# Sums of squares of the RMS norms: columns of TensorE products, in place of running additions on VectorE and GpSimd

## The chip, the core and the metric

The kernel runs on one core of a Trainium2 chip. The metric is the device time of one execution in microseconds; a kernel's time is the median of several runs. The engines are called as in the profile: PE (TensorE), PEld (its weight loads), DVE (VectorE), ACT (ScalarE), POOL (GpSimd), and SP, whose queue issues nearly all loads.

## What is computed

Two layers over 1024 latent tokens of width 1024, with 256 context tokens. Only the opening matters here: both token streams are normalised by their root mean square, then scaled and shifted by vectors that come from two conditioning vectors.

```python
def rmsnorm(x, g):
    xf = x.astype(jnp.float32)
    y = xf * lax.rsqrt(jnp.mean(xf * xf, axis=-1, keepdims=True) + RMS_EPS)
    return (y * g.astype(jnp.float32)).astype(x.dtype)
...
shift, scale, gate = jnp.split(sc @ mod_w[l] + mod_b[l], 3, axis=-1)
hx = modulate(rmsnorm(x, norm_g[l]), shift[:, None], scale[:, None])
...
shift_c, scale_c, gate_c = jnp.split(scc @ mod_w[l] + mod_b[l], 3, axis=-1)
hc = modulate(rmsnorm(ctx, norm_g[l]), shift_c, scale_c)
```

## The kernel before

Everything is held transposed: the 1024 features lie on 8 tiles of 128 partitions, the tokens along the free axis. `x_0` to `x_7` are 128x1024 tiles (two halves of 512 tokens); the context fills `cx_0` and `cx_1`, each four features' tiles of 256 tokens side by side. A sum over features is thus a sum over the 8 tiles and then over the partitions.

The opening does four things at once. (1) `fold`: PE multiplies two groups of the second layer's weights; each group has four pieces (0 to 3) of 24 products of 128x512 per column half. A weight piece is loaded (`wr_wu`), cast by ACT to `wh_wu` (L95) and its rest formed by POOL in `wl_wu` (L96); ACT copies the result out (`fo`, L254) and SP stores it. `gh` and `gl` are the group's other operand; those of the second group take the buffers of the first. (2) `modulation(k)`: DVE forms scale and shift of tile k as dot products of loaded rows `mod` (L212, L216, L220); PE forms those of tiles 6 and 7 (`mod_row`: products `modr`, L322, and transposes `modt`, L328). (3) The sums of squares. (4) `modulate(k)`: DVE multiplies each half of x by the scale and by the reciprocal root (L338), ACT adds the shift into `h0h` (L341), and DVE forms the rest `h0l` (L342). After that PE starts the first projection, `xb` (L126 to L128), which reads `h0h` and `h0l` of all eight tiles; the rest of the program follows from there.

The sums of squares before: ACT squares every half of a tile (L298, into one of four buffers `t`). The halves 0 are added to `ssq0` by POOL, the halves 1 to `ssq1` by DVE (L299); the context's eight pieces of 256 tokens are all added to `ssqc` by POOL. For x, `rstd_cols` then takes the sum over partitions as columns: four PE products with one column of `ones` as the moving operand (L193) put 128 tokens each on the partitions; ACT takes the root and DVE the reciprocal of 128x4 numbers; DVE spreads them on a diagonal `dg_x` (L197), and a product with `ones` (L200) brings them back along the free axis, the same on each partition. For the context, `rstd` multiplies `ones` by `ssqc` (L181), and takes root and reciprocal on 128x256 (L183, L184); `ctx_scale` multiplies `cx` by it (L382), POOL scales and shifts it (L349) and it is split for the projection `xbc`.

The code is not the order of execution: when the program is built, a scheduler places the instructions of each engine by its own estimate of time, and every engine then runs its list in that order. Loads (`load`) are chained, so they are issued in the order of the code. All products in float32 (those with `ones`, `modr`, `modt`) show two records per product in the trace, those in the rounded type one.

Of the kernel before, what the change touches and what calls it, by code (L numbers as in the profile page):

```python
# [9 lines left out]
F32 = mybir.dt.float32  # L10
F32R = mybir.dt.float32r
AF = mybir.ActivationFunctionType
# [3 lines left out]
P = 128  # L16
S = 1024
C = 256
E = C + S
D = 1024  # L20
KT = D // P
H = 512
HALF = (slice(0, H), slice(H, S))
# [32 lines left out]
def body(ctx, tc, xT, ctxT, cc, ccol, modT, modW, win, gw, wout, wu, grp, wg, wo1, small, edge, ident, outT):  # L56
    nc = tc.nc
    mult, add, sub = ALU.mult, ALU.add, ALU.subtract
# [19 lines left out]
    def xtile(name, dt=F32):  # L78
        return xpool.tile([P, S], dt, tag="x", name=name)

    def ttile(name):
        return tpool.tile([P, H], F32, tag="t", name=name)

    def atile(name):
        return apool.tile([P, NR * PW], F32, tag="acc", name=name)

    def psum(name):
        return pm.tile([P, H], F32, tag="mm", name=name)


    def wide(name, n):
        return pc.tile([P, S], F32, tag=("cv", "xb")[n % 2], name=name)
# [8 lines left out]
    def load(out, src):  # L101
        with ExitStack() as lctx:
            if chain[0] is not None:
                lctx.enter_context(tc.issue_after(chain[0].ins))
            d = nc.sync.dma_start(out, src)
            if chain[0] is not None:
                chain[0] = d
# [36 lines left out]
    ones = base.tile([P, P], F32, name="ones")  # L144
    nc.vector.memset(ones, 1.0 / D)
    eps_r = base.tile([P, 1], F32, name="eps_r")
# [31 lines left out]
    def rstd(acc, eps, name, wn=0):  # L178
        n = acc.shape[-1]
        ps = psum(f"ms_{name}") if n < H else wide(f"ms_{name}", wn)  # L180
        nc.tensor.matmul(ps[:, :n], ones, acc, start=True, stop=True)  # L181
        rt = ttile(f"sq_{name}")
        nc.scalar.activation(rt[:, :n], ps[:, :n], AF.Sqrt, bias=eps)  # L183
        nc.vector.reciprocal(acc, rt[:, :n])  # L184


    def rstd_cols(acc, name, idD, rpool, wn):
        n = acc.shape[-1]
        nt = n // P
        ps = wide(f"ms_{name}", wn)  # L190
        r = rpool.tile([P, H // P], F32, tag="rc", name=f"rc_{name}")[:, :nt]
        for c in range(nt):
            nc.tensor.matmul(ps[:, c : c + 1], acc[:, c * P : (c + 1) * P], ones[:, 0:1], start=True, stop=True)  # L193
        nc.scalar.activation(r, ps[:, :nt], AF.Sqrt, bias=eps_r)
        nc.vector.reciprocal(r, r)
        t = ttile(f"dg_{name}")[:, :n]
        nc.vector.tensor_tensor(out=t.rearrange("p (c t) -> p c t", t=P),  # L197
                                in0=idD.unsqueeze(1).to_broadcast([P, nt, P]),
                                in1=r.unsqueeze(2).to_broadcast([P, nt, P]), op=mult)
        nc.tensor.matmul(ps[:, H : H + n], ones, t, start=True, stop=True)  # L200
        return ps[:, H : H + n]
# [66 lines left out]
    with ExitStack() as sctx:  # L268
        fpool = sctx.enter_context(tc.tile_pool(name="fpool", bufs=6))
        gpool = sctx.enter_context(tc.tile_pool(name="gpool", bufs=4))  # L270
        spool = sctx.enter_context(tc.tile_pool(name="spool", bufs=1))
# [14 lines left out]
        cx = [spool.tile([P, D], F32, name=f"cx_{i}") for i in range(2)]  # L286


        xs = []
        acc = [atile("ssq0"), atile("ssq1")]  # L290
        accc = spool.tile([P, C], F32, name="ssqc")

        def sumsq(acc_, v, n, first, name, eng):
            if first:
                nc.scalar.activation(acc_[:, :n], v, AF.Square)
            else:
                q = ttile(name)
                nc.scalar.activation(q[:, :n], v, AF.Square)  # L298
                eng.tensor_tensor(out=acc_[:, :n], in0=acc_[:, :n], in1=q[:, :n], op=add)  # L299

        junk = spool.tile([P, D], F32, name="junk")

        def modulation(k):
            for m in (k, KT + k):
                raw = dtile(f"mod0_{m}")
                load(raw, modT[0, m])
                mod_tile(m0, 0, m, raw, (cL, cC), junk)
            mod_scale(m0, a0, 0, k)
# [3 lines left out]
        idx = spool.tile([P, P], F32, name="idx")  # L312
# [43 lines left out]
        def x_load(k):  # L356
            t = xtile(f"x_{k}")
            load(t, xT[k])
            xs.append(t)
            for h in range(2):  # L360
                sumsq(acc[h], t[:, HALF[h]], H, k == 0, f"xsq_{k}_{h}", nc.vector if h else nc.gpsimd)

        for i in range(2):
            chain[0] = nc.sync.dma_start(cx[i][:1], cc[i : i + 1])
# [3 lines left out]
        for i, t in enumerate((cL, cC)):  # L368
            ps = wide(f"c_{i}", i)
# [2 lines left out]
            nc.scalar.activation(t, ps, AF.Silu, scale=float(D))  # L372
        def ctx_load(i):
            load(cx[i].rearrange("p (k n) -> p k n", n=C), ctxT[4 * i : 4 * i + 4].rearrange("k p n -> p k n"))
            for q4 in range(4):
                sumsq(accc, cx[i][:, q4 * C : (q4 + 1) * C], C, i + q4 == 0, f"csq_{i}_{q4}", nc.gpsimd)

        def ctx_scale():
            rstd(accc, eps_r, "c")
            for i in range(2):  # L380
                v = cx[i].rearrange("p (k n) -> p k n", n=C)
                nc.vector.tensor_tensor(out=v, in0=v, in1=accc.unsqueeze(1).to_broadcast([P, 4, C]), op=mult)  # L382

        def ctx_split(i):
            for k in range(4 * i, 4 * i + 4):
# [13 lines left out]
        modulation(1)  # L399
        x_load(7)  # L400
        modulation(2)
        rx = [rstd_cols(acc[h][:, :H], f"x{h}", idx, spool, h) for h in range(2)]
        mod_row(1)
        mod_row(0)
        fold_some(2)
# [15 lines left out]
        ctx_load(0)  # L421
        fold_some(1)
        ctx_load(1)
        ctx_scale()
        ctx_split(0)
        ctx_split(1)
# [3 lines left out]
    with ExitStack() as actx:  # L430
# [95 lines left out]
        for j in range(KT):  # L526
            uc = utile(f"uc{j}")

            for src, dst in zip(xb, (uc[:, :C], uc[:, C:])):
                n = src.shape[-1]  # L530
                nc.scalar.activation(dst, src, AF.Identity, bias=col(O_SCB + j), scale=col(O_SCW + 4 * j + 2))
                for k, o in ((0, -2), (1, -1), (3, 1)):
                    a, b = max(0, -o), n - max(0, o)
# [7 lines left out]
            roots, root = (None, None) if state is None else decays(j - 1, state[1])  # L541
            w = wload(win[KT + j], f"vg{j}", nc.gpsimd)
            sg = []
            for h in range(2):
                ps = psum(f"vg{j}_{h}")
                mm3(ps, w, (hh, hl), HALF[h])
                t = ttile(f"sg{j}_{h}")
# [51 lines left out]
    def vtile(name):  # L599
        return vpool.tile([P, H], F32, tag="v", name=name)  # L600
# [16 lines left out]
    def block_sums(b11, b12, b21, b22, t3, eng):  # L617
        eng.tensor_tensor(out=t3, in0=b22, in1=b12, op=sub)
        eng.tensor_tensor(out=b12, in0=b12, in1=b11, op=sub)
        eng.tensor_tensor(out=b11, in0=b22, in1=b12, op=sub)  # L620
        eng.tensor_tensor(out=b21, in0=b21, in1=b11, op=sub)
        return dict(t2=b11, t1=b12, t3=t3, t4=b21, b22=b22)
# [94 lines left out]
    for j in range(KT):  # L717
        w = wload(win[4 * KT + j], f"gb{j}", nc.gpsimd)
        th, tl = d2tile(f"ybh{j}", F32R), d2tile(f"ybl{j}", F32R)
        for h in range(2):  # L720
            ps = psum(f"gb{j}_{h}")
# [49 lines left out]
    for h in range(2):  # L771
        ps = wide(f"mu{h}", h)[:, :H]
        nc.tensor.matmul(ps, ones, lnacc[h][:, :H], start=True, stop=True)
        for j in range(KT):
            v = us[j][:, HALF[h]]
# [177 lines left out]
    for i in range(KH):  # L953
# [3 lines left out]
        t = block_sums(b11, b12, b21, b22, ttile(f"xt3_{i}"), nc.vector)  # L957
# [105 lines left out]
    for m in range(0, NK, 2):  # L1063
# [38 lines left out]
        elif m <= KT:  # L1102
            n = 2 * KT + m - 2
# [187 lines left out]
    wb, _, _ = last_half0(m, wa, ahead)  # L1291
# [4 lines left out]
    first, second = slice(H, H + H // 2), slice(H + H // 2, S)  # L1296
# [26 lines left out]
    q4 = p3(m, wa, c4, whole, HALF[1])  # L1323
# [108 lines left out]
```

## Time and profile before

| | |
|---|---|
| time, median of 3 runs | 1375.69 us (1374.39 to 1378.43) |
| profiled execution, its own time | 1381.07 us |
| its span in the profile | 1379.3 us |
| its mean granted PE clock | 0.974 |
| PE busy | 1295.9 us (94%) |
| DVE busy | 1205.1 us (87%) |
| ACT / POOL busy | 632.7 us (46%) / 363.3 us (26%) |
| first `fold` product / first `xb` product starts | 13.32 us / 93.25 us |

The opening is thus the first 7% of the span. Durations below are those of the one profiled execution, which took 5.4 us more than the median. Where a table gives busy time in a window it also gives the clock that PE was granted there, 1.00 for full and 0.50 for half.

### The profile page before, as it was taken

Reading aid. Unit: us, or ns where it says so; the run is one execution under the profiler, and the core shown is the slowest. Engines: PE = TensorE matmul, PEld = TensorE weight load, DVE = VectorE, ACT = ScalarE, POOL = GpSimd, SP = SyncE. Lnnn points to the kernel's source line nnn. Section 1 sums busy time; section 2 is a strip of 40 time slices with the busy share of each in tenths; the row PEclk is TensorE's granted clock in tenths of the full one; section 3 lists DMA queues with packets and bytes.
Section 4 is the critical chain, followed back from the end, with each engine's and each line's share of the span. In section 5 each row is a group of like instructions: output and inputs, shape, how many; then the busy total and the mean of one; then the engine's idle time right before and its main releaser. Section 6 shows DMA issues by size and latency. Waiting matters only on the chain.

```text
span 1379.3 us, 15637 instructions
## 1 busy us (share of the span) xinstructions
PE 1295.9 (94%) x5664; PEld 1048.2 (76%) x5664; DVE 1205.1 (87%) x1587; ACT 632.7 (46%) x906; POOL 363.3 (26%) x182
## 2 busy tenths in 40 slices
PE   7889989898999799999998999999999999999896
PEld 4468868787777587787887887788888888778685
DVE  7998999999999999998778865999999987876775
ACT  6353644674465542304533544754334344634442
POOL 5173534743473555523320004000000000000002
PEclk9899999999999899999999999999999999999997
DMA  9753011111112113343353646424243334758623
GB/s 354 280 180 119 25 59 54 53 40 61 54 35 72 46 46 130 110 151 135 103 185 122 221 154 205 138 93 151 100 145 123 115 115 132 265 190 275 206 107 123
DMA packets 82866, 181.79 MB, mean 132 GB/s; under 512 B 7778, under 2 KB 27618, under 8 KB 82788
## 3 DMA queue, kind: packets, MB, share of 16 engines
q1 hardware_dynamic: 74340, 176.60, 37.8%
q10 hardware_dynamic: 8448, 4.20, 1.0%
q8 instruction: 44, 0.72, 0.2%
q14 instruction: 34, 0.28, 0.1%
HBM read 136.72 MB, written 44.04 MB: 131 GB/s over the span
## 4 chain that ended last, share of the span: by engine, by line
PE 36%; DVE 10%; DMA 7%; issue 2%; ACT 2%; POOL 1%; POOLq 0%; SPq 0%; DVEq 0%; ACTq 0%
PE ga L127 2%; PE ga L128 2%; PE ga L126 2%; PE wob L127 2%; PE wob L128 2%; PE wob L126 2%; DMA wr_g<-wg 1%; DVE ws L986 1%; DMA yr_t<-y_t 1%; DMA wr_v<-wfold 1%; PE qb_g L666 1%; DVE wq_g L96 1%; PE qb_g L669 1%; PE qb_g L668 1%; DVE wq_wo L96 1%
## 5 line engine op out<-in xcount | busy, mean ns | idle before, releaser
L746 DVE SCALAR_TENSOR_TENSOR conv<-u,sm,conv 128x1013 f32<-128x1013 f32 (+14 forms) x232 | 291.2, 1272 | 6.6 <-ACT conv L738 3.8
L1252 POOL TENSOR_TENSOR o<-x,rr 128x256 f32<-128x256 f32 (+1 forms) x9 | 8.0, 923 | 462.9 <-ACT rr L1240 460.0
L511 ACT ACTIVATE g<-g,sm 128x512 f32<-128x512 f32 (+1 forms) x96 | 58.8, 617 | 110.5 <-PE g L510 108.3
L96 POOL TENSOR_TENSOR wl_wu<-wr_wu,wh_wu 128x1024 fp32r<-128x1024 f32 x16 | 39.4, 2470 | 153.9 <-ACT wh_wu L95 147.7
L463 POOL TENSOR_TENSOR g<-g,uc 128x1280 f32<-128x1280 f32 x16 | 47.5, 2967 | 107.9 <-ACT g L511 65.1
L249 PE MATMUL fold<-gh,wh_wu 128*128 128x512 f32 x128 | 53.0, 416 | 5.7 <-ACT wh_wu L95 5.7
L250 PE MATMUL fold<-gl,wh_wu 128*128 128x512 f32 x128 | 52.4, 409 | 3.2 <-DVE gl L96 3.2
L128 PE MATMUL gb<-h0h,wl_gb 128*128 128x512 f32 x128 | 50.7, 398 | 4.8 <-POOL wl_gb L96 4.8
L126 PE MATMUL vg<-h0h,wh_vg 128*128 128x512 f32 x128 | 52.3, 408 | 2.7 <-ACT g L511 2.1
L251 PE MATMUL fold<-gh,wl_wu 128*128 128x512 f32 x128 | 50.7, 405 | 2.3 <-POOL wl_wu L96 2.3
L128 PE MATMUL xb<-h0h,wl_xb 128*128 128x512 f32 x128 | 50.2, 392 | 2.0 <-POOL wl_xb L96 2.0
L127 PE MATMUL wob<-ybl,wh_wob 128*128 128x512 f32 x128 | 50.5, 395 | 1.2 <-POOL ybl L96 1.2
L465 POOL TENSOR_TENSOR g<-g,th 128x1280 f32<-128x1280 f32 x16 | 46.9, 2948 | 16.8 <-ACT th L449 16.8
L127 PE MATMUL vg<-h0l,wh_vg 128*128 128x512 f32 x128 | 51.2, 400 | 0.0
L126 PE MATMUL gb<-h0h,wh_gb 128*128 128x512 f32 x128 | 50.6, 395 | 0.1
L126 PE MATMUL va<-h0h,wh_va 128*128 128x512 f32 x128 | 50.6, 395 | 0.0
L127 PE MATMUL va<-h0l,wh_va 128*128 128x512 f32 x128 | 50.6, 395 | 0.0
L508 PE MATMUL g<-uh,wh_gw 128*128 128x512 f32 (+1 forms) x96 | 36.3, 379 | 15.1 <-ACT wh_gw L95 6.4
L126 PE MATMUL wob<-ybh,wh_wob 128*128 128x512 f32 x128 | 50.6, 396 | 0.0
L128 PE MATMUL wob<-ybh,wl_wob 128*128 128x512 f32 x128 | 49.9, 391 | 0.7 <-POOL wl_wob L96 0.7
L128 PE MATMUL va<-h0h,wl_va 128*128 128x512 f32 x128 | 50.4, 395 | 0.0
L127 PE MATMUL gb<-h0l,wh_gb 128*128 128x512 f32 x128 | 50.4, 393 | 0.0
(548 smaller groups left out, 4301.1 us busy)
## 6 DMA issues: line engine op xcount, KB each, us to landing
mod<-modT SPq DMA_DIRECT2D x28, 512.0 KB, 5.5
wr_wu<-wu SPq DMA_DIRECT2D x16, 512.0 KB, 3.9
x_part<-xp SPq DMA_DIRECT2D x32, 256.0 KB, 2.4
mod<-modT SPq DMA_DIRECT2D x32, 256.0 KB, 3.3
wr_v<-wfold SPq DMA_DIRECT2D x16, 512.0 KB, 3.7
wr_g<-wg SPq DMA_DIRECT2D x16, 512.0 KB, 5.4
wr_wo<-wo SPq DMA_DIRECT2D x16, 512.0 KB, 4.2
yr_t<-y_t SPq DMA_DIRECT2D x16, 512.0 KB, 6.3
```

The costliest lines, as they stand in the source:

```text
L96: eng.tensor_tensor(out=lo, in0=src, in1=hi.bitcast(F32), op=sub))
L126: nc.tensor.matmul(ps, hi[:, kc], xh[k][:, cols], start=(k == 0), stop=False)
L127: nc.tensor.matmul(ps, hi[:, kc], xl[k][:, cols], start=False, stop=False)
L128: nc.tensor.matmul(ps, lo[:, kc], xh[k][:, cols], start=False, stop=(k == ks - 1))
L249: nc.tensor.matmul(ps, wh[:, kc], gh[i], start=(i == 0), stop=False)
L250: nc.tensor.matmul(ps, wh[:, kc], gl[i], start=False, stop=False)
L251: nc.tensor.matmul(ps, wl[:, kc], gh[i], start=False, stop=(i == 3))
L463: nc.gpsimd.tensor_tensor(out=ius[d], in0=ius[d], in1=uc, op=mult)
L465: nc.gpsimd.tensor_tensor(out=ius[d], in0=ius[d], in1=roots[d], op=mult)
L508: nc.tensor.matmul(ps[:, :n], gwh[:, kc], uh[:, a : a + n], start=True, stop=False)
L511: nc.scalar.activation(t[:, a : a + n], ps[:, :n], AF.Sigmoid, bias=col(ob + d * KT + j))
L746: nc.vector.scalar_tensor_tensor(out=(us[j] if k == 30 else acp)[:, a:b], in0=us[j][:, a + o : b + o], scalar=col(O_CONVW + 31 * j + k), i ...
```

## The change

The running sums `ssq0`, `ssq1` and `ssqc` and their additions are gone. Each squared half goes straight to PE: for each 128 tokens of it one product with one column of `ones`, into a column of its own of one PSUM tile (`sumsq`): 64 columns for x (`ms_x`, 8 per tile) and 16 for the context (`ms_c`). `roots` copies half of the columns out of PSUM by ACT, halves them three times by additions on DVE (128x32, 128x16 and 128x8 results for x; 128x8, 128x4, 128x2 for the context), and takes root and reciprocal. `spread` is the old diagonal and the product with `ones`; the context now goes that way as well, and its squares are taken in four pieces of 512 instead of eight of 256. The factor for the context is read from PSUM.

```diff
-        acc = [atile("ssq0"), atile("ssq1")]
-        accc = spool.tile([P, C], F32, name="ssqc")
-
-        def sumsq(acc_, v, n, first, name, eng):
-            if first:
-                nc.scalar.activation(acc_[:, :n], v, AF.Square)
-            else:
-                q = ttile(name)
-                nc.scalar.activation(q[:, :n], v, AF.Square)
-                eng.tensor_tensor(out=acc_[:, :n], in0=acc_[:, :n], in1=q[:, :n], op=add)
+        colsums = {}
+
+        def sumsq(ps, col0, v, name):
+            q = ttile(name)
+            n = v.shape[-1]
+            nc.scalar.activation(q[:, :n], v, AF.Square)
+            for c in range(n // P):
+                nc.tensor.matmul(ps[:, col0 + c : col0 + c + 1], q[:, c * P : (c + 1) * P], ones[:, 0:1],
+                                 start=True, stop=True)
+
+        def roots(ps, nt, name):
+            a = spool.tile([P, KT // 2 * nt], F32, name=f"cs_{name}")
+            b = spool.tile([P, KT // 2 * nt], F32, name=f"ct_{name}")
+            n = KT // 2 * nt
+            nc.scalar.copy(a, ps[:, :n])
+            nc.vector.tensor_tensor(out=a, in0=a, in1=ps[:, n : 2 * n], op=add)
+            nc.vector.tensor_tensor(out=b[:, : n // 2], in0=a[:, : n // 2], in1=a[:, n // 2 : n], op=add)
+            nc.vector.tensor_tensor(out=a[:, :nt], in0=b[:, :nt], in1=b[:, nt : 2 * nt], op=add)
+            nc.scalar.activation(b[:, :nt], a[:, :nt], AF.Sqrt, bias=eps_r)
+            nc.vector.reciprocal(b[:, :nt], b[:, :nt])
+            return b[:, :nt]
+
+        def spread(ps, r, name):
+            nt = r.shape[-1]
+            t = ttile(f"dg_{name}")[:, : nt * P]
+            nc.vector.tensor_tensor(out=t.rearrange("p (c t) -> p c t", t=P),
+                                    in0=idx.unsqueeze(1).to_broadcast([P, nt, P]),
+                                    in1=r.unsqueeze(2).to_broadcast([P, nt, P]), op=mult)
+            nc.tensor.matmul(ps, ones, t, start=True, stop=True)
+            return ps
...
+            if k == 0:
+                colsums["x"] = wide("ms_x", 0)
             for h in range(2):
-                sumsq(acc[h], t[:, HALF[h]], H, k == 0, f"xsq_{k}_{h}", nc.vector if h else nc.gpsimd)
+                sumsq(colsums["x"], k * (S // P) + h * (H // P), t[:, HALF[h]], f"xsq_{k}_{h}")
...
-            for q4 in range(4):
-                sumsq(accc, cx[i][:, q4 * C : (q4 + 1) * C], C, i + q4 == 0, f"csq_{i}_{q4}", nc.gpsimd)
+            if i == 0:
+                colsums["c"] = psum("ms_c")
+            for h in range(2):
+                sumsq(colsums["c"], (2 * i + h) * (H // P), cx[i][:, HALF[h]], f"csq_{i}_{h}")

         def ctx_scale():
-            rstd(accc, eps_r, "c")
+            ps = colsums["c"]
+            rc = spread(ps[:, C:], roots(ps, C // P, "c"), "c")
...
-        rx = [rstd_cols(acc[h][:, :H], f"x{h}", idx, spool, h) for h in range(2)]
+        rt = roots(colsums["x"], S // P, "x")
+        rx = [spread(ps[:, HALF[1]], rt[:, h * (H // P) : (h + 1) * (H // P)], f"x{h}")
+              for h, ps in enumerate((colsums["x"], wide("ms_x1", 1)))]
```

The scheduler places the new products, and moves others around them. From the `vg` projection on, the lists of all engines are the same but for a few neighbours that change places.

PE, at the end of fold piece 0 (`fold_0_...`, the number behind is the column half), before:

```order
L251 MATMUL fold_0_1_248<-gh_1_211,wl_wu_0_229 128x512
L249 MATMUL fold_1_0_298<-gh_0_205,wh_wu_1_294 128x512
L250 MATMUL fold_1_0_298<-gl_0_206,wh_wu_1_294 128x512
L249 MATMUL fold_1_1_314<-gh_0_205,wh_wu_1_294 128x512
L250 MATMUL fold_1_1_314<-gl_0_206,wh_wu_1_294 128x512
L249 MATMUL fold_2_0_336<-gh_0_205,wh_wu_2_332 128x512
```

The same place after; `xsq` is a squared half, and x4 stands for the four 128-token columns of it:

```order
L251 MATMUL fold_0_1_245<-gh_1_208,wl_wu_0_226 128x512
L298 MATMUL ms_x<-ones,xsq_0_278 128x1 x4
L298 MATMUL ms_x<-ones,xsq_1_284 128x1 x4
L298 MATMUL ms_x<-ones,xsq_0_292 128x1 x4
L298 MATMUL ms_x<-ones,xsq_1_298 128x1 x4
L249 MATMUL fold_1_0_324<-gh_0_202,wh_wu_1_320 128x512
L250 MATMUL fold_1_0_324<-gl_0_203,wh_wu_1_320 128x512
L251 MATMUL fold_1_0_324<-gh_0_202,wl_wu_1_321 128x512
```

Sixteen products of x_1 and x_2 now run as one train between the pieces; eight of x_0 stand inside piece 0 and eight of x_3 six products further on.

PE, at the end of fold piece 2, before (`modr` is the conditioning product, `modt` its transpose):

```order
L251 MATMUL fold_2_1_352<-gh_1_211,wl_wu_2_333 128x512
L193 MATMUL ms_x_422<-ones,ssq_184 128x1 x4
L193 MATMUL ms_x_433<-ones,ssq_185 128x1 x4
L322 MATMUL modr_444<-modw_0_445,ccv 2x256 x4
L200 MATMUL ms_x_422<-dg_x_430,ones 128x512
L322 MATMUL modr_444<-modw_1_451,ccv 2x256 x4
L200 MATMUL ms_x_433<-dg_x_441,ones 128x512
L328 MATMUL modt_459<-idx,modrow_457 128x2 x2
```

After:

```order
L298 MATMUL ms_x<-ones,xsq_0_396 128x1 x4
L298 MATMUL ms_x<-ones,xsq_1_402 128x1 x4
L298 MATMUL ms_x<-ones,xsq_0_410 128x1 x4
L298 MATMUL ms_x<-ones,xsq_1_416 128x1 x4
L344 MATMUL modr_487<-modw_0_488,ccv 2x256
L298 MATMUL ms_x<-ones,xsq_0_424 128x1 x4
L298 MATMUL ms_x<-ones,xsq_1_430 128x1 x4
L298 MATMUL ms_x<-ones,xsq_0_449 128x1 x4
L298 MATMUL ms_x<-ones,xsq_1_455 128x1 x4
L344 MATMUL modr_487<-modw_0_488,ccv 2x256 x3
L344 MATMUL modr_487<-modw_1_494,ccv 2x256 x4
L320 MATMUL ms_x<-dg_x_481,ones 128x512
```

Where eight one-column products stood there are now 32, of x_4 to x_7, with one `modr` product between; the product that spreads the root stands behind all eight products of the first `modr` row. On DVE the diagonal now stands behind `modulation(4)`, which before came after the first x tiles were scaled.

PE, in the first half of the first projection, tiles 5 and 6, before:

```order
L126 MATMUL xb_826<-h0h_637,wh_xb_821 128x512
L127 MATMUL xb_826<-h0l_638,wh_xb_821 128x512
L128 MATMUL xb_826<-h0h_637,wl_xb_822 128x512
L126 MATMUL xb_826<-h0h_643,wh_xb_821 128x512
L127 MATMUL xb_826<-h0l_644,wh_xb_821 128x512
```

After:

```order
L126 MATMUL xb_878<-h0h_680,wh_xb_873 128x512
L320 MATMUL ms_c<-dg_c,ones 128x256
L127 MATMUL xb_878<-h0l_681,wh_xb_873 128x512
L128 MATMUL xb_878<-h0h_680,wl_xb_874 128x512
L126 MATMUL xb_878<-h0h_686,wh_xb_873 128x512
```

The context's product with `ones` stood before fold piece 3 of the second group; now the context's spread stands behind the first 16 products of `xb`, and its diagonal `dg_c` stands on DVE behind the last `h0l`.

More of the change, by code (lines that the diff above doesn't have):

```diff
@@ L374, in ctx_load @@
             load(cx[i].rearrange("p (k n) -> p k n", n=C), ctxT[4 * i : 4 * i + 4].rearrange("k p n -> p k n"))
-            for q4 in range(4):
-                sumsq(accc, cx[i][:, q4 * C : (q4 + 1) * C], C, i + q4 == 0, f"csq_{i}_{q4}", nc.gpsimd)
+            if i == 0:
+                colsums["c"] = psum("ms_c")
+            for h in range(2):
+                sumsq(colsums["c"], (2 * i + h) * (H // P), cx[i][:, HALF[h]], f"csq_{i}_{h}")
         def ctx_scale():
-            rstd(accc, eps_r, "c")
+            ps = colsums["c"]
+            rc = spread(ps[:, C:], roots(ps, C // P, "c"), "c")
             for i in range(2):
                 v = cx[i].rearrange("p (k n) -> p k n", n=C)
-                nc.vector.tensor_tensor(out=v, in0=v, in1=accc.unsqueeze(1).to_broadcast([P, 4, C]), op=mult)
+                nc.vector.tensor_tensor(out=v, in0=v, in1=rc.unsqueeze(1).to_broadcast([P, 4, C]), op=mult)
         def ctx_split(i):
```

## The prediction

> **What bounds the kernel now.** I read the page's engine totals and chain first, then the opening by windows, then PE's waits there, and last the rows of the operations that come and go. The page:
>
> ```profile
> span 1379.3 us, 15637 instructions
> PE 1295.9 (94%) x5664; PEld 1048.2 (76%) x5664; DVE 1205.1 (87%) x1587; ACT 632.7 (46%) x906; POOL 363.3 (26%) x182
> PE 36%; DVE 10%; DMA 7%; issue 2%; ACT 2%; POOL 1%; POOLq 0%; SPq 0%; DVEq 0%; ACTq 0%
> ```
>
> PE is busy 94% of the span and leads the chain that ended last. Only the opening changes, so the question is when PE reaches the first projection `xb`. Two chains meet there:
>
> ```profile
> 93.25 0.39 PE L126 MATMUL xb<-h0h,wh_xb 128*128 128x512 f32 x1
> 93.55 4.51 DVE L342 SCALAR_TENSOR_TENSOR h0l<-x,m,h0h 128x1024 fp32r<-128x1024 f32 x2
> 97.99 2.35 DVE L382 TENSOR_TENSOR cx<-cx,ssqc 128x1024 f32<-128x1024 f32 x2
> ```
>
> PE ends its folds at 93.25; DVE ends the last `h0l` at 98.06, and PE needs it for product 23 of `xb`, at 93.25 + 22 x 0.22 = 98.1 (0.22 us a product, below). Behind that the lists are alike, so I carry a shift of this point to the end one for one. Neither chain can shorten the opening alone. First PE's (windows: from:to, length, then PE, PEld, DVE, ACT, POOL busy with counts, granted PE clock, DMA share, GB/s; most are cut at the steps of the clock):
>
> ```profile
> 13.30:93.20 79.90, 66.13 (x254) 45.79 (x255) 75.36 (x104) 40.98 (x63) 44.55 (x23) 0.91 0.76 268
> 20.40:23.80 3.40, 0.86 (x5) 0.40 (x3) 2.77 (x4) 2.69 (x5) 1.30 (x2) 1.00 1.03 398
> 23.80:27.20 3.40, 3.40 (x8) 2.64 (x9) 1.00 (x1) 3.40 (x6) 3.40 (x2) 0.51 1.02 413
> 37.40:40.90 3.50, 1.92 (x13) 1.39 (x14) 3.47 (x7) 1.27 (x2) 0.00 (x0) 1.00 1.03 419
> 40.90:44.30 3.40, 2.62 (x6) 0.76 (x4) 3.40 (x9) 0.26 (x1) 0.00 (x0) 0.51 1.03 398
> 44.30:47.70 3.40, 3.40 (x8) 0.72 (x7) 3.40 (x10) 0.00 (x0) 0.00 (x0) 0.50 0.98 273
> 61.30:64.80 3.50, 0.83 (x4) 0.70 (x5) 3.47 (x7) 0.35 (x1) 0.00 (x0) 1.00 0.97 334
> 64.80:68.20 3.40, 3.40 (x10) 2.64 (x9) 3.37 (x8) 0.00 (x0) 0.00 (x0) 0.50 0.01 2
> 85.30:88.70 3.40, 1.74 (x7) 1.18 (x8) 3.33 (x7) 1.78 (x4) 3.32 (x4) 1.00 0.00 0
> 88.70:92.10 3.40, 3.40 (x15) 2.81 (x16) 3.40 (x4) 1.84 (x3) 2.18 (x1) 1.00 0.62 181
> ```
>
> Of 79.9 us PE is busy 66.1. The clock moves in steps of 3.4 us: a window with little PE work is followed by one at half clock (23.8, 40.9, 64.8), and 44.3 stays at half because 40.9 was not full. That is four half windows, 4 x 3.4 x 0.5 / 79.9 = 0.09 below 1, as the first row's 0.91 says. The pair to note is 85.3 and 37.4: almost the same busy time (1.74 and 1.92), but the first, filled with 512-wide folds, keeps the clock and the second, filled half with the eight one-column products and half with `modr`, loses it. So PE time in such products counts for less than its length. PE's waits in the same 80 us:
>
> ```profile
> PE fold L249 <- ACT wh_wu L95: 5.7, 3, 2.7
> PE fold L250 <- DVE gl L96: 3.2, 1, 3.2
> PE fold L251 <- POOL wl_wu L96: 2.3, 3, 1.2
> PE ms_c L181 <- POOL ssqc L299: 2.2, 1, 2.2
> PE ms_x L193 <- DVE ssq L299: 1.7, 1, 1.7
> PE ms_x L200 <- DVE m L216: 0.8, 1, 0.8
> PE modt L328 <- ACT modrow L325: 0.5, 1, 0.5
> ```
>
> The longest of the first row, 2.7, ends at 13.3 and stays. The rest is 16.4 - 2.7 = 13.7 us, room that PE can fill.
>
> **The change, part by part.** The rows that price it (group rows: count, busy us, mean ns, idle before; then single rows: start, us; then two windows):
>
> ```profile
> L193 PE MATMUL ms_x<-ones,ssq 128*128 128x1 f32 x16 | 2.0, 245 | 1.7 <-DVE ssq L299 1.7
> L299 DVE TENSOR_TENSOR ssq<-ssq,xsq 128x512 f32<-128x512 f32 x7 | 9.7, 1379 | 3.1 <-ACT xsq L298 2.9
> L299 POOL TENSOR_TENSOR ssq<-ssq,xsq 128x512 f32<-128x512 f32 x7 | 12.9, 1840 | 1.9 <-ACT xsq L298 1.6
> L299 POOL TENSOR_TENSOR ssqc<-ssqc,csq 128x256 f32<-128x256 f32 x7 | 9.8, 1395 | 0.4
> L184 DVE RECIPROCAL ssqc<-sq_c 128x256 f32<-128x256 f32 x1 | 1.7, 1739 | 0.0
> L197 DVE TENSOR_TENSOR dg_x<-idx,rc_x 128x512 f32<-128x512 f32 x2 | 1.4, 685 | 0.0
> L195 DVE RECIPROCAL rc_x<-rc_x 128x4 f32<-128x4 f32 x2 | 0.3, 169 | 0.0
> L194 ACT ACTIVATE rc_x<-ms_x,eps_r 128x4 f32<-128x4 f32 x2 | 0.5, 264 | 4.6 <-DVE m L216 4.6
> ```
> ```profile
> 24.23 0.63 PE L250 MATMUL fold<-gl,wh_wu 128*128 128x512 f32 x1
> 24.65 0.63 PE L249 MATMUL fold<-gh,wh_wu 128*128 128x512 f32 x1
> 28.17 0.39 PE L249 MATMUL fold<-gh,wh_wu 128*128 128x512 f32 x1
> 28.39 0.39 PE L250 MATMUL fold<-gl,wh_wu 128*128 128x512 f32 x1
> 36.33 0.95 PE L193 MATMUL ms_x<-ones,ssq 128*128 128x1 f32 x8
> 1363.65 0.61 PE L1225 MATMUL fin_ms<-ones,fin 128*128 128x1 f32 x4 [1.36 <-DVE fin L1217]
> 1366.29 1.01 PE L1225 MATMUL fin_ms<-ones,fin 128*128 128x1 f32 x4 [2.03 <-DVE fin L1217]
> 1363.65:1364.25 0.60, 0.60 (x4) 0.52 (x4) 0.60 (x2) 0.00 (x0) 0.60 (x1) 1.00 0.00 0
> 1366.30:1367.20 0.90, 0.90 (x5) 0.90 (x5) 0.87 (x3) 0.00 (x0) 0.00 (x0) 0.50 1.03 375
> ```
>
> *One-column products on PE.* A float32 product is two records (8 products, x16), and eight records take 0.95 us at 36.33, 0.12 us a record. x: 64 products are 128 records, 16 of them there before: +112 x 0.12 = 13.4 us. Context: 16 products, 32 records: +3.8 us. The spreads of x stay, and that of the context has the size of the product it replaces: 0. Sum **+17.2 us** of PE work at full clock. At half clock they are slower, too (four in 1.01 us against 0.61, late in the program, where the last two rows give the clock); that is inside the price of a half window below.
>
> *PE's waits.* 13.7 us of room as above. I take all of it as filled: POOL's 12.9 + 9.8 us of additions leave, so `wl_wu` and the context's sum are no longer late, and a PE that is behind finds `gl`, `wh_wu` and `modrow` ready. Net 17.2 - 13.7 = **+3.5 us**. If the 3.2 us for `gl` remain, since DVE still forms them behind three `h0l`, it is +6.7; that end goes into the range.
>
> *Half-clock windows.* In one, a 512-wide product starts every 0.42 us (24.65 - 24.23) against 0.22 (28.39 - 28.17), so 3.4 us do the work of about 1.7: each costs 1.7 us, and there were four. The train of 16 products of x_1 and x_2 is 32 x 0.12 = 3.8 us, longer than a window, so one window at least goes low, and the eight of x_3 only six folds later may hold the clock down once more: 1 or 2 half windows, I take 1.5. The train of 32 (x_4 to x_7) is 64 x 0.12 = 7.7 us: the second window of it is at half clock at the latest, what is left of the train (2.6 us) doubles to some 5 us, and then `modr`, which before could not lift the clock for two windows after only eight such products, takes two more: about 4. Together **5.5 instead of 4: +1.5 x 1.7 = 2.6 us**. The eight products of x_0 and the two pairs of trains of the context, 1.9 us each between folds, cost none. Bounds: 0 half windows, if the trains count as full work (-4 x 1.7 = -6.8), and 10 (+10.2), if each train costs one or two more than I give it.
>
> *DVE.* Seven additions leave, 9.7 us; the context's reciprocal of 1.7 us becomes one of 128x2. Eight small operations come, at 0.17 us each by the row of the 128x4 reciprocals, and `dg_c` at half of 0.685: 9.7 + 1.7 - 1.4 - 0.3 = 9.7 us less work. The time gains nothing by that: in the sum PE arrives later than DVE. `modulation(4)` moves ahead of the diagonal; DVE would wait there for its rows `mod`, and then for PE's last train. Both hide behind PE, which runs eight `modr` products between train and spread; without that cover the chain of copy, three additions, root, reciprocal and diagonal (0.26 + 4 x 0.17 + 0.26 + 2 x 0.685, 2.6 us) would show.
>
> *The new wait.* The context's spread stands in PE's list behind 16 products of `xb`, and waits for `dg_c` behind the last `h0l`: behind it wait the other 32 products of `xb`, and DVE's scaling of `cx`, POOL's eight steps and the split. After `h0l` come three additions, root, reciprocal, diagonal: 4 x 0.17 + 0.26 + 0.34, 1.3 us, and the hand-overs between them, which I estimate at 0.2. Before, `h0l` ended 98.06 - (93.25 + 16 x 0.22) = 1.3 us after that place. With DVE 9.7 us lighter and PE 6 us later it is covered, 0; with neither it is 2.8. I take 0.
>
> *ACT, POOL, SP.* ACT squares as before, in four pieces for the context instead of eight; two copies of 128x32 and 128x8 come, under 0.3 us each by the 128x4 row. Its squares now wait for PE to read one of the four buffers `t`, with the cast of the next weight piece queued behind; that is late only where PE is. POOL only loses work. On SP the stores of `fo_0_0` and `fo_0_1` move behind loads issued after 32 us, long after piece 0 ends; the loads of the later `mod` rows stand behind the stores of piece 2 as before. 0.
>
> **Sum**: 17.2 - 13.7 + 2.6 = +6.1 us: 1381.07 + 6.1 = 1387.2 for the profiled execution's own time. That one lies 5.4 above the median, so against the median of the runs, 1375.69 + 6.1 = **1381.8 us**.
>
> **Rivals.** *The trains count as work, and the clock stays up* (0 or 1 half window). For it: PE issues them without a gap. Against it: the pair of windows above. Then 17.2 - 13.7 - 6.8 = -3.3 us, or -1.6 with one: 1372.4 to 1374.1, not slower. It decides where a window filled with trains keeps 1.00. The Trainium skill, "TensorE: Matmul & The Clock Gate", section "Part 1: The HAM clock gate", says the clock falls after an idle window of about 3.4 us, and trains leave no idle one, so by that rule the sum would be the -3.3 us of this rival. This trace is stricter than that rule: 20.4 and 61.3 lost the clock with 0.86 and 0.83 us of work in them, and 37.4 with 1.92.
>
> *The trains count for a part* (2 to 4 half windows): 17.2 - 13.7 - 1.7 x (0 to 2) = 0.1 to +3.5, 1375.8 to 1379.2.
>
> *Everything is late* (7 windows or more, or `gl` or the new wait shows on top): +3.5 + 3 x 1.7 = +8.6 and, with the 2.8 of that wait, +11.4: 1384 to 1387.
>
> *DVE's relief decides*: POOL's additions held DVE up (its own seven additions took 1.38 us each, `dg_x` of the same size 0.69), and both chains shorten. PE's list must still fit, so beyond -3.3 us it needs records cheaper than 0.12: about -5, 1370.7.
>
> **Numbers.** About 0.3% (4.1 us) is what a measurement can tell from no change here. Chances: 5 to 6 half windows, the forecast, 0.38 (own range 1380 to 1384); all late 0.12; part-counting 0.22; clock stays up 0.20; DVE's relief 0.08. Faster by over 0.3%: 0.08. Within: 0.22 + 0.20 = 0.42. Slower: 0.50. The range leaves out the last rival and the end of the late one: 1371.8 to 1386.5.
>
> **What would show it.** After: about 160 one-column records, 0.12 us apart at full clock; no DVE or POOL row with `ssq`; granted clock of 0.50 after the train behind piece 0 and during the train behind piece 2, and some 5 half windows before the first `xb` product, which starts near 99; PE's waits in the opening under 4 us. Wrong: a granted clock of 1.00 through the trains, with `xb` near 90; or a long wait of PE at the context's spread.

## The result, and the profile after

The changed kernel takes 1382.7 us (median of 9, 1379.0 to 1387.7) against 1375.7 for the kernel before (9 runs beside it): ratio 1.0053, 95% interval 1.0032 to 1.0073, so 4.4 to 10 us slower. The forecast was 1381.8. Its profiled execution took 1386.2 us. The page, the lines that answer to those of before:

```profile
span 1384.3 us, 15894 instructions
PE 1313.6 (95%) x5808; PEld 1068.6 (77%) x5808; DVE 1190.2 (86%) x1586; ACT 633.1 (46%) x903; POOL 343.6 (25%) x168
DVE 13%; PE 10%; DMA 8%; issue 2%; ACT 2%; POOL 0%; SPq 0%; POOLq 0%; DVEq 0%; ACTq 0%
```

PE has 17.7 us more busy time, DVE 15 less, POOL 20 less. The chain now names DVE first. That says little: in a second execution of this kernel PE has 45% of it, and behind the opening every engine's list is row for row that of before. The opening by windows (columns as before), whole and then cut at the steps of the clock:

```profile
13.30:101.67 88.37, 87.49 (x397) 69.46 (x397) 63.42 (x99) 41.02 (x59) 24.77 (x9) 0.86 0.67 241
24.70:28.10 3.40, 3.40 (x32) 3.40 (x32) 2.20 (x1) 2.98 (x5) 2.36 (x1) 1.00 1.02 408
28.20:31.60 3.40, 3.40 (x12) 2.81 (x12) 3.33 (x7) 0.61 (x1) 0.00 (x0) 0.50 1.02 405
31.60:35.00 3.40, 3.40 (x14) 3.21 (x15) 3.33 (x9) 1.26 (x2) 0.00 (x0) 0.50 1.02 406
35.00:38.40 3.40, 3.40 (x9) 2.63 (x9) 3.26 (x9) 0.59 (x1) 0.00 (x0) 0.50 1.06 402
45.20:48.60 3.40, 3.40 (x32) 3.32 (x30) 3.37 (x3) 2.08 (x4) 2.87 (x1) 1.00 0.73 176
48.60:52.00 3.40, 3.40 (x16) 2.53 (x15) 0.89 (x4) 1.96 (x3) 0.71 (x1) 0.51 0.91 361
52.00:55.40 3.40, 3.40 (x18) 3.40 (x17) 0.00 (x0) 0.00 (x0) 1.64 (x1) 0.50 1.02 411
55.40:58.80 3.40, 3.40 (x14) 2.39 (x15) 0.53 (x3) 1.33 (x2) 0.00 (x0) 0.50 1.06 376
58.80:62.20 3.40, 3.40 (x9) 1.02 (x8) 1.50 (x3) 0.43 (x2) 0.00 (x0) 0.50 0.21 67
62.30:65.70 3.40, 3.40 (x13) 1.45 (x12) 1.65 (x3) 0.36 (x1) 0.00 (x0) 1.00 0.00 0
```

PE is busy 87.5 of 88.4 us, so the 13.8 us of waiting have shrunk to 0.9. The clock is printed as 0.86: half clock from 28.2 to 38.4 (three windows) and from 48.6 to 62.2 (four), in both cases right behind a window in which PE was busy for all of 3.40 us, with columns (one-column products). Seven half windows, where there were four.

One stretch is missing from that column, here and in the kernel before: it prints 1.00 where the profile has no record of the clock yet, and the records begin at 21.3 us (before: at 17.0). Up to there PE ran at half clock, too. The folds start 0.42 to 0.43 us apart ahead of that point, and 0.23 to 0.24 behind it (start, us; the first five rows are of the changed kernel, the last four of the kernel before):

```profile
15.18 3.41 PE L298 MATMUL ms_x<-ones,xsq 128*128 128x1 f32 x16
20.30 0.63 PE L249 MATMUL fold<-gh,wh_wu 128*128 128x512 f32 x1
20.73 0.63 PE L250 MATMUL fold<-gl,wh_wu 128*128 128x512 f32 x1
21.47 0.40 PE L249 MATMUL fold<-gh,wh_wu 128*128 128x512 f32 x1
21.70 0.40 PE L250 MATMUL fold<-gl,wh_wu 128*128 128x512 f32 x1
16.38 0.63 PE L249 MATMUL fold<-gh,wh_wu 128*128 128x512 f32 x1
16.80 0.51 PE L250 MATMUL fold<-gl,wh_wu 128*128 128x512 f32 x1
17.16 0.40 PE L251 MATMUL fold<-gh,wl_wu 128*128 128x512 f32 x1
17.40 0.40 PE L249 MATMUL fold<-gh,wh_wu 128*128 128x512 f32 x1
```

So behind the first fold at 13.3 stand 8.0 us more at half clock, and 3.7 in the kernel before (8.2 and 5.7 in the second profile of each). The eight products of x_0 lie in them. "Half windows" below are the recorded ones; this start is given beside them.

What PE waits for from 13 us to the first `xb`, and what DVE waits for in the same time:

```profile
PE fold L249 <- ACT wh_wu L95: 2.7, 1, 2.7
PE modt L350 <- ACT modrow L347: 0.5, 1, 0.5
PE fold L250 <- DVE gl L96: 0.4, 1, 0.4
DVE junk L212 <- DMA mod<-modT: 10.9, 2, 7.4
DVE cs_x L307 <- ACT cs_x L306: 8.1, 1, 8.1
DVE x L360 <- PE ms_x L320: 3.2, 1, 3.2
```

DVE's two waits for rows `mod` end at 25.9 and 42.0, ahead of its wait for the last train of x, which ends at 57.7; that wait would otherwise be longer. The rows of the timeline (start, us):

```profile
24.45 3.63 PE L298 MATMUL ms_x<-ones,xsq 128*128 128x1 f32 x32
45.55 4.00 PE L298 MATMUL ms_x<-ones,xsq 128*128 128x1 f32 x32
50.42 6.99 PE L298 MATMUL ms_x<-ones,xsq 128*128 128x1 f32 x32
57.34 5.61 PE L344 MATMUL modr<-modw,ccv 128*2 128x256 f32 x14
62.88 1.98 PE L320 MATMUL ms_x<-dg_x,ones 128*128 128x512 f32 x4
101.67 0.39 PE L126 MATMUL xb<-h0h,wh_xb 128*128 128x512 f32 x1
105.99 0.67 PE L320 MATMUL ms_c<-dg_c,ones 128*128 128x256 f32 x2 [0.32 <-DVE dg_c L317]
98.57 5.82 DVE L364 SCALAR_TENSOR_TENSOR h0l<-x,m,h0h 128x1024 fp32r<-128x1024 f32 x3
```

A train of 32 records takes 3.63 us at full clock, 4.00 where its last 0.9 us fall into half clock (from 48.6), and 6.99 at half. The spread of x stands at 62.9, behind the trains and eight `modr` products, where before DVE began to scale x at 46.3. The first `xb` starts at 101.67, 8.4 us later than before; the last `h0l` ends at 104.4, ahead of its use.

### The profile page after: what moved, and what is told of

It is laid out like the page before. It is cut to its first block, busy times and chain, and to the rows that moved or that the text cites. A ratio compares the mean times of both kernels' runs of the same rounds, so it can differ in the third digit from the quotient of the medians.

```text
span 1384.3 us, 15894 instructions
## 1 busy us (share of the span) xinstructions
PE 1313.6 (95%) x5808; PEld 1068.6 (77%) x5808; DVE 1190.2 (86%) x1586; ACT 633.1 (46%) x903; POOL 343.6 (25%) x168
## 5 line engine op out<-in xcount | busy, mean ns | idle before, releaser
L96 POOL TENSOR_TENSOR wl_wu<-wr_wu,wh_wu 128x1024 fp32r<-128x1024 f32 x16 | 42.3, 2647 | 180.3 <-ACT wh_wu L95 158.1
L95 ACT CAST wq_wo<-wr_wo 128x512 fp32r<-128x512 f32 x48 | 28.8, 619 | 49.8 <-DMA wr_wo<-wo 19.9
```

What stands on the lines that cost most here:

```text
L95: return (nc.scalar.copy(hi, src), eng.tensor_tensor(out=lo, in0=src, in1=hi.bitcast(F32), op=sub))
L96: eng.tensor_tensor(out=lo, in0=src, in1=hi.bitcast(F32), op=sub))
```

## The experiments

All versions in one table. Half windows are the recorded ones between 13 us and the first `xb` in the profile; "start" is the time at half clock, in us, from the first fold to the first record of the clock; `va` is the first projection whose list is alike in all of them, 117.97 us in the kernel before. "Same lists" says whether the engines' lists behind the opening are those of before; the scheduler lays some of them otherwise although no code there differs.

| version | half windows | start | first `xb` | last `h0l` ends | first `va` | same lists | median | ratio to before, 95% |
|---|---|---|---|---|---|---|---|---|
| before | 4 | 3.7 | 93.25 | 98.1 | 117.97 | | 1375.7 | 1 |
| changed | 7 | 8.0 | 101.67 | 104.4 | 127.59 | yes | 1382.7 | 1.0053 (1.0032 to 1.0073) |
| changed, again | 7 | 8.2 | 101.84 | 104.6 | 127.77 | yes | 1381.3 | 1.0054 (1.0040 to 1.0068) |
| + 56 wide products | 0 | 10.1 | 104.65 | 107.4 | 130.59 | yes | 1387.0 | 1.0082 (1.0058 to 1.0105) |
| + 32 wide products | 8 | 9.8 | 111.12 | 113.9 | 137.03 | yes | 1395.3 | 1.0149 (1.0125 to 1.0172) |
| + 64 wide products | 0 | 11.3 | 106.27 | 109.0 | 132.20 | no | 1394.9 | 1.0148 (1.0131 to 1.0165) |
| columns for x only | 7 | 8.8 | 105.22 | 112.3 | 132.27 | yes | 1391.8 | 1.0103 (1.0073 to 1.0132) |
| columns for context only | 2 | 6.3 | 90.63 | 93.3 | 115.80 | no | 1377.9 | 1.0000 (0.9985 to 1.0016) |
| x by wide float32 | 1 | 2.9 | 96.21 | 100.0 | 121.49 | no | 1383.3 | 1.0047 (1.0027 to 1.0066) |
| x by wide rounded | 4 | 5.3 | 94.47 | 98.7 | 121.02 | no | 1378.5 | 1.0021 (1.0005 to 1.0038) |
| the same, early spread | 4 | 5.9 | 93.04 | 87.4 | 118.21 | no | 1378.5 | 1.0029 (1.0015 to 1.0043) |
| the same, `gl` on POOL | 4 | 4.6 | 95.30 | 93.5 | 121.22 | but for a few rows | 1378.7 | 1.0024 (1.0005 to 1.0042) |

Each ratio is to runs of the kernel before made beside the version. Their medians differ a little from row to row: 1377.2 for x only, context only and float32; 1375.4 for the changed kernel again, 64 products, rounded and early spread; 1376.4 for 56, 32 and `gl` on POOL. The start is 8.0 us or longer in all six rows with columns for x, and 6.3 or shorter in the others: the train of x_0 is part of what keeps the clock down there.

The theory to test (clock theory): columns are PE work, and for the clock they hardly count as work, so the trains bring the half windows. Rivals: they are work and no more (work theory), or the loss sits in the moved instructions (list theory).

**What the clock counts, by itself.** PE alone, stretches of one kind behind one another:

```diff
+    for c in range(128):
+        column(c)
+    heat(90)
+    for wides, columns, n in ((1, 4, 24), (1, 2, 36), (1, 1, 60), (2, 1, 40)):
+        for q in range(n):
+            for _ in range(wides):
+                mm(mix, wr, xr)
+            for c in range(columns):
+                column(c)
+        heat(90)
```

> This kernel computes nothing of the reference: PE alone runs stretches of products behind one another, each between two stretches of 90 wide products (128x512, rounded type, 0.23 us each at full clock). First 128 one-column products (256 records); then mixes of one wide product with 4, 2 and 1 columns and of two wide with one column; then 30 float32 products of 128x512; then 80 products of the shape of modr (2x256). Clock theory (columns keep PE busy but count little as work for the clock): granted clock 0.50 in the column stretch from its second window of 3.4 us at the latest, with 0.12 us a record at full and some 0.22 at half clock, about 50 us for 256 records; the mix 1:4 (19% of the time in wide products) at half clock, 1:1 (49%) and 2:1 (66%) at full, 1:2 (32%) undecided; the float32 wide products at full clock. Work theory (the clock falls only where PE waits): 1.00 in all stretches, 256 records in 31 us.

Windows over the column stretch, the mixes 1:4, 1:2 and 1:1, the float32 wide products, and the products of the shape of `modr`:

```profile
28.38:80.30 51.92, 51.92 (x257) 51.92 (x256) 0.00 (x0) 0.00 (x0) 0.00 (x0) 0.53 0.00 1
103.36:151.80 48.44, 48.44 (x217) 46.28 (x216) 0.00 (x0) 0.00 (x0) 0.00 (x0) 0.53 0.00 1
175.00:215.30 40.30, 40.30 (x181) 37.36 (x180) 0.00 (x0) 0.00 (x0) 0.00 (x0) 0.58 0.00 0
237.50:264.60 27.10, 27.10 (x181) 24.65 (x180) 0.00 (x0) 0.00 (x0) 0.00 (x0) 1.00 0.00 1
333.00:358.90 25.90, 25.90 (x62) 11.53 (x61) 0.00 (x0) 0.00 (x0) 0.00 (x0) 1.00 0.00 0
379.30:414.00 34.70, 34.70 (x162) 13.58 (x161) 0.00 (x0) 0.00 (x0) 0.00 (x0) 1.00 0.00 0
```

PE is busy all the time in every row, and the clock is still 0.53 and 0.58 in the first three: full in the first window or two, half to the end of the stretch. The work theory falls here. One wide product per two columns (5.0 wide products per 3.4 us at full clock: the groups start 0.68 us apart) is too little; one per column (7.5) is enough. `modr` products, 256 wide, hold the clock.

The Trainium skill, "TensorE: Matmul & The Clock Gate", section "Part 1: The HAM clock gate", gives the slow clock to a PE that was idle for a window. These rows differ from that, with no idle time in 52 us, nearly all of them at half clock; the measurement decides.

**The same in the program.** Wide products that nobody reads (their moving operand is all zeros), in the trains of the changed kernel:

```diff
             for c in range(n // P):
-                nc.tensor.matmul(ps[:, col0 + c : col0 + c + 1], ...)
+                mm = nc.tensor.matmul(ps[:, col0 + c : col0 + c + 1], ...)
+                if "x" in name and c % 2 == 0 and name[4] != "0":     # 56; 32: no name[4], range(1); 64: every c, range(1)
+                    for _ in range(2):
+                        with tc.issue_after(mm.ins):
+                            mm = nc.tensor.matmul(colsums["d"][:, :H], onesr, dumb, start=True, stop=True)
```

> The changed kernel with one more product, 128x512 in the rounded type and read by nobody, behind each one-column product of x: 64 x 0.23 = 14.6 us more PE work, and trains that spend about half their time in wide products. Clock theory: at that share the clock stays up (the mix 1:1 alone stayed at full clock), so the 7 half windows of the opening fall to 2 or less, 8.5 us back: +6 us on the changed kernel, first xb near 108, time near 1389. Work theory (the half windows have another cause than the trains): +14.6 us, first xb near 116, time near 1397. If VectorE, not PE, ends the opening in the changed kernel: as the clock theory or less, since the spread of x comes later by what the trains grow.

> The changed kernel with two of the wide products that nobody reads behind every other column of x_1 to x_7: 56 x 0.23 = 12.7 us more PE work at the same share of about one half, and from the end of the opening on every engine's list is that of the changed kernel row for row, which it was not with 64 of them. Clock theory: 0 or 1 half window in the opening in place of 7, 10 to 12 us back, first xb 1 to 3 us later than in the changed kernel, time 1383 to 1386. Work theory: first xb near 114, time near 1394. If the other lists behind the opening, and not the opening, made the version with 64 slow, this one comes out near 1385; if the opening made it slow, near 1393.

> As before it, but one wide product behind every other column of all eight tiles: 32 x 0.23 = 7.3 us more PE work, about a third of a train's time, and the same lists behind the opening. Clock theory: a third is too little for a long train (the mix 1:2 alone fell to half clock in its second window), so 2 to 5 half windows remain: first xb between 100 and 106, time 1380 to 1387. If one wide product per two columns were enough: no half window, first xb near 98, time near 1379. Work theory: 7.3 us more than the changed kernel, first xb near 109, time near 1389.

The opening up to the first `xb`, with 56 and with 32:

```profile
13.30:104.65 91.35, 90.22 (x452) 72.75 (x453) 63.94 (x99) 41.53 (x60) 24.82 (x9) 1.00 0.64 232
13.30:111.10 97.80, 96.93 (x428) 77.83 (x429) 61.40 (x99) 41.35 (x59) 24.45 (x9) 0.86 0.60 217
```

With 56 every recorded window is at 1.00 (the records begin at 23.7): 12.7 us more work, and `xb` only 3.0 us later. With 32 there are eight half windows, and `xb` is 9.5 us later. So 24 more products, 5.5 us of work, bring `xb` 6.5 us earlier and make the program 8.3 us faster (1387.0 against 1395.3; the lists behind the opening are the same, and in both the train of x_3 joined that of x_1 and x_2). That is the clock theory in the program itself, and its expected numbers for 56 (`xb` 1 to 3 us later; time 1 above its 1383 to 1386), where the work theory had 1394. For 32 the clock theory expected 2 to 5 half windows; eight came: these trains are longer, but not dense enough, and last more windows. Its time lies above the 1389 of the work theory, too. The version with 64 has its `xb` where the clock theory had it or 1.7 earlier, but a time 6 us above the expected 1389, nearer to the 1397 of the work theory; its lists behind the opening differ, which is taken up below.

**Which half of the change.** Columns for x alone, and for the context alone:

```diff
+            for q4 in range(4):      # x only: the context as before
+                sumadd(accc, cx[i][:, q4 * C : (q4 + 1) * C], C, i + q4 == 0, f"csq_{i}_{q4}", nc.gpsimd)
+            rstd(accc, eps_r, "c")
...
+            for h in range(2):       # context only: x as before
+                sumadd(acc[h], t[:, HALF[h]], H, k == 0, f"xsq_{k}_{h}", nc.vector if h else nc.gpsimd)
+        rx = [rstd_cols(acc[h][:, :H], f"x{h}", idx, spool, h) for h in range(2)]
```

> Columns for x alone; the context keeps its additions on POOL and its product with ones before the last fold piece. Clock theory: the trains behind pieces 0 and 2 are as before, so 7 half windows stay, and only 3.8 us of columns leave while some 2 us of waiting for the context's sum come back: first xb near 100, time 2 us under the changed kernel, some 1380 to 1381. List theory (the loss sits in the context's spread behind 16 xb products and in its diagonal behind the last h0l): that place is as in the kernel before, so the time is within 2 us of it, 1374 to 1378. Work theory: 13.4 us of work less 13.7 us of room: within 2 us of the kernel before.

> Columns for the context alone; x keeps its additions on POOL and DVE. Clock theory: 4 half windows as before, 3.8 us of columns between folds less the 2.2 us of waiting for the context's sum: +1 to +2 us, 1376 to 1378. List theory: most of the 7 us stays, 1380 to 1383. Work theory: +1 to +4, 1376 to 1380.

The seven half windows stay with x, as expected, and the context's columns bring none (1377.9, within the expected 1376 to 1378). But x alone is 14.6 us slower than the kernel before beside it, where both together are 7.0 slower, which no theory had. PE's waits there, then a row of DVE and of POOL:

```profile
PE xb L126 <- DVE x L369: 2.5, 1, 2.5
PE fold L251 <- POOL wl_wu L96: 2.4, 2, 1.4
PE xb L127 <- DVE h0l L373: 1.9, 1, 1.9
98.45 2.35 DVE L216 TENSOR_TENSOR m<-m,sm 128x2 f32<-128x2 f32 x1
97.40 3.38 POOL L96 TENSOR_TENSOR wl_xb<-wr_xb,wh_xb 128x1024 fp32r<-128x1024 f32 x1
```

The late spread has moved DVE's chain of `h0l` to the end of the opening. With the context's additions still on POOL, which delay its `wl` pieces to just there, DVE's 128x2 operation stands 2.35 us beside POOL's 128x1024 one (0.15 in the changed kernel), the reciprocal of 128x256 is back, and the last `h0l` ends 8 us later. The twelve operations of this kind (L216) take 4.4 us more than in the changed kernel and the reciprocal 1.7, some 6 of the 8; this is read from the rows and was not tried by itself. The list theory gets no support: with the context's place of before the time does not come back, and with columns for the context alone under 1 us of the 7 stays. Neither version is a clean test of it, since each brings something new: late waits in the first, other lists in the second.

**Wide products for the sums.** `ones` as the stationary operand, squares moving:

```diff
-            for c in range(n // P):
-                nc.tensor.matmul(ps[:, col0 + c : col0 + c + 1], q[:, c * P : (c + 1) * P], ones[:, 0:1], ...)
+            nc.tensor.matmul(ps, ones, q, start=first, stop=last)   # rounded: q and ones in F32R
...
+        with tc.issue_after(rx_mm[0].ins):                          # early spread: modr behind it
+            mod_row(1)
...
-            split(raw, th, tl, nc.vector)
+            split(raw, th, tl, nc.vector if g != 1 else nc.gpsimd)  # gl on POOL, half of modr ahead of the spread
```

> As the changed kernel, but the sums of x are taken with ones as the stationary operand and the squares moving, 512 wide, one float32 product per half of a tile (16), added up over the tiles in PSUM; eight one-column products turn the row of sums into columns. PE work is about the same: 16 products of two records of some 0.5 us, 16 us, in place of 128 records of 0.12, 15.4 us. Clock theory: wide products count as work, so the half windows fall from 7 to 3 or 4, 5 to 7 us less than the changed kernel: 1376 to 1378, first xb near 96. Work theory: as the changed kernel or 1 us more, 1382 to 1384. List theory: as the changed kernel, since the context's place is the same.

> Sums of x by wide products as in the float32 version, but in the rounded type: squares written rounded, one record of 0.23 us each, 16 x 0.23 = 3.6 us in place of 15.4; context as in the changed kernel. Work and clock theory together: 12 us less PE work than with float32 wide products and 1 to 3 half windows, so PE has waits again and VectorE's chain from the spread of x to the last h0l ends the opening: with the spread 5 us earlier than in the float32 version, first xb at 88 to 92, time 1372 to 1376, 1 to 5 us under the kernel before. If the last h0l does not come earlier with the spread (VectorE bound by something else): first xb near 96, time 1378 to 1382.

> As the version with rounded wide products, and PE's list holds both rows of modr behind the spreads of x instead of ahead of them; PE then waits some 2 us ahead of the spreads for root, reciprocal and diagonal, and VectorE gets the factor of x about 5 us earlier. The context's spread falls behind the first 2 products of xb. If VectorE's chain behind the spread sets the end: the last h0l comes 3 to 5 us earlier than with rounded wide products alone, time 1368 to 1373. If PE's list sets it, or PE waits at the context's spread for its diagonal: the same as rounded wide products alone or up to 4 us more, 1374 to 1380.

> Sums of x by rounded wide products, the spreads of x behind half of the first modr row, gl of the second group formed by GpSimd, which has nothing else to do there, context as in the changed kernel. Behind the opening the lists are those of the kernel before but for a few neighbours. VectorE's chain has 10 us of slack by then, so PE sets the end of the opening: the 3.5 us of waiting for gl go, and with them one or two half windows: first xb at 86 to 90, time 1368 to 1373, 3 to 7 us under the kernel before. If waits and half windows only move to another place: first xb 92 to 94, time 1374 to 1377, no change.

In float32 the opening has one half window in place of seven with about the same PE work, and `xb` starts at 96.2 as the clock theory said. The time did not follow (1383.3, expected 1376 to 1378; the work theory had 1382 to 1384, from an opening as late as the changed kernel's, which it is not); its lists behind the opening differ. In the rounded type some 10 us of work less bring `xb` only to 94.5: PE then waits 4.7 us for `gl` and has four half windows, as before the change. The early spread frees DVE (last `h0l` at 87.4), but PE, no longer held up by DVE, still arrives at 93.0. `gl` on POOL was to remove a wait of 3.5; instead PE waits 2.1 for `gl`, 2.0 for `wl_wu` and 1.1 for `fo`, and `xb` starts at 95.3. None of these beats the kernel before; the expected 1372 to 1376 failed, and 1368 to 1373 twice.

**Both kernels again.**

> The changed kernel again, for a second profile and for times beside the three below. All theories: +5 to +8 us on the kernel before, first xb between 100 and 102, 6 or 7 half windows before it.

> The kernel before once more, for a second profile of its opening. If the opening does not hang on where the 3.4 us windows of the clock happen to fall: first xb within 0.5 us of 93.3 and 4 half windows. If it does: 2 to 5 half windows, first xb between 90 and 95.

The changed kernel repeats: seven half windows, `xb` at 101.84. Before repeats too: `xb` at 92.94 and four half windows, at 39.7, 43.1, 63.5 and 73.8 instead of 23.8, 40.9, 44.3 and 64.8. The windows fall elsewhere in each execution; their number is the same here, and `xb` is within 0.3 us.

## Why the prediction was right

The time came out 0.9 us from the forecast, and its direction was that of the likeliest case. The mechanism holds: PE's waits are filled, the columns are work, and half clock comes on top. The sizes of the terms are off both ways, and that the sum came so near is partly luck. Step by step:

- *One-column products*, +17.2 us at 0.12 us a record. Measured 0.113 at full clock and 0.218 at half: the price was right, and 144 records are 16.3 us. All of PE's work up to the first `xb`, counted at full clock, grew by less: 13.4 us (below). What makes the difference was not taken apart; one part is the context's product with `ones`, which now stands behind the first products of `xb`.
- *PE's waits*, 13.7 us filled. They went from 13.8 to 0.9, so 12.9 are filled; `gl` went from 3.2 to 0.4 and did not stay.
- *Half-clock windows*, 5.5 instead of 4. This term was mis-sized: seven, in both profiles. The train of x_4 to x_7 cost the four it was given. The trains of x_1 to x_3 cost three, not 1.5: the eight products of x_3 (30.5 to 33.9) fall into the first two half windows, and a third follows. +5.1 us in place of +2.6. The eight products of x_0, which were to cost none, stand in the half clock at the start, which the prediction's table prints as 1.00 and its count of four leaves out; that start is 8.0 us instead of 3.7.
- *The sum at `xb`*. Between first fold and first `xb` PE is busy 87.5 us, 31.9 of them at half clock, against 66.2 and 16.2 before. Counted at full clock that is 71.5 us of work against 58.1, and 16.0 us lost by half clock against 8.1. So +13.4 - 12.9 + 7.9 = +8.4, which is what was measured, against 17.2 - 13.7 + 2.6 = 6.1 (the second profiles of both kernels: +13.0 - 10.7 + 6.6 = +9.0). The forecast's "near 99" was 2.7 us too early. By the number of half windows the opening is that of the rival "everything is late".
- *Carried one for one*. `va` is 9.6 and 9.8 us late, the medians 7.0 and 5.9. By the other versions with the same lists the step holds within about 2 us: x only 14.3 and 14.6, 56 wide products 12.6 and 10.6, 32 wide products 19.1 and 18.9 (`va` and median, against before beside them). So 2 to 4 us of the delay are missing behind the opening, and they set off the half clock that was counted too low: the number is partly right by this. In the mean clocks of all executions (records only) the changed kernel has 20.2 half windows against 18.4 (0.9750 of 14, 0.9772 of 62, each (1 - clock) x span / (0.5 x 3.41)): some 1.8 more in the whole program with three more in the opening, so about one fewer behind it. Why, is not settled.
- *DVE 9.7 us lighter, no gain*: right (11.9 us lighter up to `xb`), but not only because PE is later. DVE lost the additions and now waits 8.1 us for the last train and 3.2 for the spread. With the context's additions left on POOL its chain is the late one, so by that version POOL's relief, booked at 0, is what keeps DVE covered.
- *The new wait* at the context's spread, 0 with 2.8 as its bound: 0.3.
- *Rivals*. The clock did not stay up; it does with the 56 wide products, at the price of their own work. DVE's relief shortened nothing.

## What to carry to other kernels

Before work is moved to TensorE in small products, ask two things of the profile: how long a record takes, and how much a window of 3.4 us moves through the array. Products that load a full 128x128 operand for one column fill PE's time and not its clock window; one wide product per column kept the clock here, one per two columns did not. The sum with the wide operand moving, in float32, left one half window of seven, but no version here was faster than the kernel before. Where the first windows of a profile print full clock, check it by the spacing of like products. What is freed on another engine is lost again if its next input stands behind the new PE work.

## What the runs showed of the hardware

- The clock does not follow PE's busy time; these cases go by how much moves per window. Kept at full: 7.5 wide products per 3.4 us (the mix 1:1), records of 256 columns at 0.22 us (the same, counted in columns). Lost: 5.0, with PE busy throughout. Whether columns are counted, or the time in products that move many, no run tells apart.
- A mix that keeps full clock need not bring it back. In the version with 64 wide products the window from 17.5 to 20.9 is nearly all mix 1:1, at half clock, and the clock rises only at 24.3; 28.2 in the changed kernel was two thirds wide products and was followed by another half window.
- Adding work can shorten a program: 24 wide products more, 8.3 us less.
- Two versions whose lists behind the opening differ from before, though no code there does, and are row for row alike in these two, took 3 us (context only) and 5 us (64 wide products) more than their `va` accounts for; the three other versions with other lists took 0 to 3 more. That the lists are the cause was not tried by itself.
- The chain of waits hangs on a single execution: PE's share of it is 10% in one profile of the changed kernel and 45% in the other.
